# Three edits to the channel sub-layer of a decoder layer: product order in the first unit, the engine of the first partial sums, and the spacing of reloaded weights

## The chip, the cores and the metric

The kernel runs on one core of one Trainium2 chip. The metric is the device time of one execution in microseconds (us). The engines of the core are TensorE (PE, with its weight loads shown as PEld), VectorE (DVE), ScalarE (ACT), GpSimd (POOL) and SyncE (SP); each works through its own queue in order, and semaphores connect them. SP, ACT and POOL also issue DMA transfers from their queues (SPq, ACTq, POOLq). A change in time of under 0.5% (about 10.5 us here) can't be told from none.

## The reference

The kernel computes one decoder layer for a prompt of 1024 tokens and for 8 samples with one token each. A mixer sub-layer (stick-breaking attention and gated linear attention) is followed by the channel sub-layer, which the change is about:

```python
h2 = modulate(x1, sh2, sc2)
f = jnp.square(jax.nn.relu(h2 @ w_ff1)) @ w_ff2
x2 = layer_norm(ALPHA * x1 + gt2 * f, ln2_g, ln2_b)
```

The model width is 1024, `w_ff1` is 1024 x 4096 and `w_ff2` 4096 x 1024, all in float32. The 8 samples attend over a paged cache of 8192 tokens each (`cache_k`, `cache_v`, 1 MB gathers), and their layer is the same one with the same weights, so each sample passes through the mixer, then through the channel sub-layer.

## The kernel before, in words

Products. A float32 product is made as three products of a rounded high part and a low part: high by high, low by high, high by low. `three(terms)` (L485) lists them for a list of terms, one kind after the other: all high by high, then all low by high, then all high by low. `mm` (L341) records every matmul, `turn` (L367) every transpose on TensorE, and one wrapper (L212) every operation of the other engines, so that nearly all rows of the profile carry one of these three lines, and tiles tell them apart.

The prompt runs through the channel sub-layer in two halves of 512 rows: `ffn(0, ...)`, then `ffn(1, ...)` (L1578). `second_in` (L1547) makes the input of a half: eight blocks h2 of 128 x 512. For each, four transposes into `pT2`, one DVE operation that writes the modulated block, an ACT operation that writes its high part, and a POOL operation that writes its low part. The hidden width of 4096 is cut into 32 units of 128 columns. `up` (L1670) multiplies the eight blocks by a unit's weights: 24 matmuls into one PSUM tile `pmm`, then ReLU on ACT (`rl`), square on DVE, and the split into `hidh` and `hidl`. Two units make a group, and `down_tile` (L1715) multiplies a group by its rows of `w_ff2`: for each of 4 row blocks t and 2 column halves cc a sum of 6 products, in the PSUM tile `pz` (cc = 0) or `ptr` (cc = 1). `add_up` (L1735) brings each such sum into the eight running sums `f[t][cc]`: the first group's by an ACT copy, the later ones by a DVE addition. The tiles `f` come from a ring of eight buffers, so the first sums of `ffn(1)` go where the finished rows of `ffn(0)` were, once these have been stored. `finish` (L1811) normalises a row block and stores it: in `ffn(0)` by DVE and a store from ACT's queue, in `ffn(1)` by POOL (for t = 3 by DVE) and a store from SP's queue.

Weights are loaded through SP's queue into a ring of six raw buffers (`raw`, `N_RAW`), split by ACT (high) and POOL (low).

The samples. Their attention over the cache runs beside all of this as small tasks: per task a 1 MB gather of keys on POOL's queue, a multiply and a reduce on DVE (`kt`, `z`), for values eight small matmuls (`va`). When it is done, their input `h2s` is made. From then on each pair of units that `ffn(1)` loads is also used for the samples (`smp_up` L1606, `smp_sum` L1595, `smp_down` L1621): 16 matmuls with a unit pair's `w_ff1` columns (`cT` in the rows), a sum over partitions (`sel`), the squared ReLU (`hs`), and 8 matmuls into the tile `pfs`. Pairs that the prompt passed before that time are missed, and `smp_late` (L1633) loads their weights again: for each missed pair two loads `wfs` of `w_ff1`, an estimated pause, two loads `wfs2` of `w_ff2`, a pause, then the products. `smp_end` (L1760) waits until all 16 pairs are summed, then copies `pfs`, multiplies by the selector, adds the residual, normalises the 8 rows `srow` and stores `out_y_sample`.

What sets the order: the program is recorded by generators that take turns under a clock of the kernel's own (`Flow`, L45; every `yield x` stands for x us, stretched by `SCALE` = 1.2). This clock runs on estimates when the program is built, and so decides in which order each engine's instructions stand, and also how many pairs count as missed (`range(u)` in `load_up`). On the chip each queue then runs in that order.

## Time and profile before

| | |
|---|---|
| three runs | 2112.74 us median (2105.89 to 2117.82) |
| the profiled execution | 2098.6 us, span of its instructions 2096.9 us |
| TensorE busy / VectorE / GpSimd / ScalarE | 93% / 71% / 42% / 34% of the span |
| mean granted TensorE clock | 0.962 |
| chain that ended last, by engine | PE 57%, DVE 17%, DMA 13%, issue 6%, ACT 4%, POOL 2% |
| reloads `wfs` and `wfs2` | 36 loads of 512 KB (18 units, nine pairs) |

How to read it: the page is of one execution, which was 14 us faster than the median of the three others; durations and places below are of that execution. `ffn(0)` begins at about 1132 us of the span, `ffn(1)` has its first sums at about 1652 us, the last prompt product ends at about 2077 us, and the span ends at 2096.9 us. In the rows of a timeline a start and a duration are followed by engine, line, operation, output<-inputs and count, and in brackets the idle time of the engine before it and what ended it.

### The profile page before, as it was taken

To read this page: it belongs to the slowest core of one execution; us is meant where nothing else is said; L and a number is where in the kernel's file an instruction comes from. 1 tells how busy PE (TensorE), PEld (TensorE's weight loads), DVE (VectorE), ACT (ScalarE), POOL (GpSimd) and SP (SyncE) were. 2 spreads that over 40 slices of the span, in tenths; PEclk is the share of its full clock that TensorE was granted. 3 is DMA by queue.
4 is the path that set the end of the run, shared out by engine and by line. 5 is a ranking of instruction groups with operands and counts; after the bars stand their busy time and mean duration, and the time that the engine had idled before them with its cause. 6 is when DMAs were issued, how large, how long until landed. Compare 5 with 4: busy or idle time off the path is not lost.

```text
span 2096.9 us, 28831 instructions
## 1 busy us (share of the span) xinstructions
PE 1942.7 (93%) x11300; PEld 1376.2 (66%) x11300; DVE 1497.7 (71%) x1796; ACT 706.6 (34%) x1152; POOL 876.4 (42%) x597
## 2 busy tenths in 40 slices
PE   5899999999999899998998889999998999999997
PEld 2676765666656676677777656767675666677774
DVE  6568877798867588667898878887897533533357
ACT  2325444454444543222322423232222522322222
POOL 2232233334323223364466536555454644323324
PEclk9899999999999799998999999999999999999998
DMA  7785678777757558897797858787886866545554
GB/s 254 249 290 172 214 244 280 273 236 253 256 198 247 180 178 315 318 329 289 241 335 246 286 211 288 262 306 256 278 299 233 274 229 212 179 122 151 151 175 149
DMA packets 279554, 506.45 MB, mean 242 GB/s; under 512 B 16261, under 2 KB 207077, under 8 KB 243578
## 3 DMA queue, kind: packets, MB, share of 16 engines
q0 software_dynamic: 36864, 268.45, 35.2%
q1 hardware_dynamic: 215010, 207.56, 31.6%
q10 hardware_dynamic: 27544, 28.59, 3.9%
q8 instruction: 89, 1.46, 0.3%
q14 instruction: 47, 0.39, 0.1%
HBM read 473.84 MB, written 30.71 MB: 241 GB/s over the span
## 4 chain that ended last, share of the span: by engine, by line
PE 57%; DVE 17%; DMA 13%; issue 6%; ACT 4%; POOL 2%; SPq 1%; ACTq 0%; DVEq 0%; POOLq 0%
PE pmm L341 23%; PE pz L341 8%; PE ptr L341 7%; PE pbig L341 6%; PE va L341 4%; DMA vt<-in_cache_v,idx 3%; DMA wf<-in_w_ff 3%; DVE kt L212 2%; DVE z L212 2%; PE pfs L341 2%; DVE f L212 2%; DVE kp L212 2%; DVE xr L212 1%; PE paT L367 1%; PE po L341 1%
## 5 line engine op out<-in xcount | busy, mean ns | idle before, releaser
L212 DVE TENSOR_TENSOR kt<-kt,qb 128x2048 f32<-128x2048 f32 x128 | 291.4, 2278 | 26.7 <-DMA kt<-in_cache_k,idx 25.7
L212 DVE TENSOR_REDUCE z<-kt 128x32 f32<-128x2048 f32 x128 | 291.8, 2281 | 1.7
L341 PE MATMUL pmm<-h,wfh 128*128 128x512 f32 x1024 | 264.4, 404 | 3.7 <-ACT h L212 3.7
L341 PEld LDWEIGHTS pmm<-h,wfh 128*128 128x128 f32 x1024 | 190.7, 190 | 78.8 <-issue 32.4
L212 POOL DMA_INDIRECT vt<-in_cache_v,idx x128 | 133.1, 1040 | 242.7 <-PE va L341 100.9
L212 POOL TENSOR_TENSOR wfl<-wf,wfh 128x1024 fp32r<-128x1024 f32 x64 | 153.9, 2405 | 179.2 <-ACT wfh L212 91.0
L212 POOL DMA_INDIRECT kt<-in_cache_k,idx x128 | 129.8, 1014 | 217.0 <-PE va L341 72.5
L212 POOL TENSOR_TENSOR wf2l<-wf,wf2h 128x1024 fp32r<-128x1024 f32 x62 | 153.0, 2478 | 129.4 <-ACT wf2h L212 120.5
L341 PE MATMUL va<-vt,wT 128*8 128x512 f32 x1024 | 140.4, 622 | 19.0 <-DMA vt<-in_cache_v,idx 18.9
L212 ACT ACTIVATE wfh<-wf 128x1024 fp32r<-128x1024 f32 x64 | 67.7, 1057 | 236.8 <-PE pmm L341 153.9
L212 DVE TENSOR_TENSOR rl<-rl,pmm 128x512 f32<-128x512 f32 x64 | 43.7, 682 | 142.6 <-ACT rl L212 142.6
L341 PE MATMUL pmm<-hhl,wbrh 128*128 128x512 f32 x512 | 141.7, 412 | 0.6 <-DVE ke L212 0.6
L341 PE MATMUL pmm<-h,wfl 128*128 128x512 f32 x512 | 132.7, 398 | 0.0
L341 PEld LDWEIGHTS pmm<-h,wfl 128*128 128x128 f32 x512 | 96.6, 190 | 28.2 <-issue 6.8
L341 PEld LDWEIGHTS pmm<-hhl,wbrh 128*128 128x128 f32 x512 | 91.8, 191 | 34.9 <-issue 18.5
L212 DVE TENSOR_TENSOR f<-f,ptr 128x512 f32<-128x512 f32 x104 | 70.9, 682 | 49.6 <-PE ptr L341 49.5
L212 DVE TENSOR_TENSOR hidl<-rl,hidh 128x512 fp32r<-128x512 f32 x64 | 83.6, 1307 | 31.7 <-ACT hidh L212 30.2
L341 PE MATMUL pz<-wf2h,hidh 128*128 128x512 f32 x248 | 85.6, 421 | 17.8 <-ACT f L212 8.5
L212 DVE TENSOR_TENSOR_SCAN kp<-kp,zcol 128x512 f32<-128x512 f32 (+3 forms) x96 | 98.8, 1043 | 2.7 <-ACT kp L212 1.7
L212 DVE TENSOR_TENSOR f<-f,pz 128x512 f32<-128x512 f32 x104 | 70.9, 681 | 36.2 <-PE pz L341 36.0
L341 PE MATMUL ptr<-wf2h,hidh 128*128 128x512 f32 x248 | 83.8, 418 | 4.5 <-DVE f L212 3.4
L212 ACT ACTIVATE rl<-pmm 128x512 f32<-128x512 f32 x64 | 38.0, 594 | 147.5 <-PE pmm L341 143.4
(376 smaller groups left out, 3972.1 us busy)
## 6 DMA issues: line engine op xcount, KB each, us to landing
wf<-in_w_ff SPq DMA_DIRECT2D x128, 512.0 KB
ra<-in_w_ada SPq DMA_DIRECT2D x24, 1024.0 KB
wfs<-in_w_ff SPq DMA_DIRECT2D x36, 512.0 KB
wbr<-in_w_in SPq DMA_DIRECT2D x16, 512.0 KB
d_br<-brg ACTq DMA_DIRECT2D x32, 256.0 KB
g<-d_br SPq DMA_DIRECT2D x32, 256.0 KB
wo<-in_w_o SPq DMA_DIRECT2D x16, 512.0 KB
xt<-in_x_prompt SPq DMA_DIRECT2D x8, 512.0 KB
```

Source lines behind the costliest of these rows:

```text
L212: ins = f(*a, **k)
L341: ins = E.matmul(out, lhsT, rhs, start=start, stop=stop, **kw)
L367: E.transpose(out, in_, idn)
```

## The change

Three edits.

1. In `smp_late` the two pauses of 10.0 per missed pair become 6.5 (12 and 7.8 us of the kernel's own clock).
2. In `up`, unit 0 of each half lists its 24 products block by block: for each of the eight blocks high by high, low by high, high by low. The other 31 units stay as they were.
3. `add_up` takes the column half cc, and the first sums with cc = 1 are copied by DVE instead of ACT.

```diff
--- before.py
+++ after.py
@@ -1635,7 +1635,7 @@
                 rs = [raw([P, 8, P], "wfs") for y in range(2)]
                 for y in range(2):
                     Y.dma_start(rs[y], w_cols(w_ff1, P * (u + y), P))
-                yield 10.0
+                yield 6.5
                 go = []
                 flow.spawn(smp_up(rs, go))
                 rs = [raw([P, 2, 512], "wfs2") for y in range(2)]
@@ -1643,7 +1643,7 @@
                     Y.dma_start(
                         rs[y], w_ff2[P * (u + y) : P * (u + y) + P, :].rearrange("p (a b) -> p a b", a=2)
                     )
-                yield 10.0
+                yield 6.5
                 yield lambda: bool(go) and until(*rs, *go)()
                 smp_down(rs, go)
                 yield 1.0
@@ -1669,7 +1669,9 @@
 
         def up(u, wh, wl):
             p = p_mm()
-            steps = three([(h2[k], (wh[:, k, :], wl[:, k, :])) for k in range(8)])
+            terms = [(h2[k], (wh[:, k, :], wl[:, k, :])) for k in range(8)]
+
+            steps = three(terms) if u else [x for y in terms for x in three([y])]
             for x, (h, wt) in enumerate(steps):
                 mm(p, wt, h, start=x == 0, stop=x == 23)
                 if x % 6 == 5 and x < 23:
@@ -1732,9 +1734,9 @@
                 yield 1.5
 
 
-        def add_up(f, p, first):
+        def add_up(f, p, first, cc):
             if first:
-                S.activation(f, p, AF.Copy)
+                V.tensor_copy(f, p) if cc else S.activation(f, p, AF.Copy)
             else:
                 V.tensor_tensor(f, f, p, ALU.add)
 
@@ -1799,7 +1801,7 @@
                         if x > NU // 2 - 3:
                             gated(f[t][cc], gt_t[cc], p)
                         else:
-                            add_up(f[t][cc], p, x == 0)
+                            add_up(f[t][cc], p, x == 0, cc)
                         yield
             if x == NU // 2 - 3 and us is not None:
                 flow.spawn(residual())
```

Since the order of the program follows the estimated clock, more rows move than these lines say. Three places follow.

On PE, at the first unit of `ffn(0)`, before (pmm_9996 and pmm_10070 are units 0 and 1, h2_9979 is the last of the eight input blocks, pT2_9972 its transposes):

```order
L341 MATMUL pmm_10070<-h2_9915,wfh_9986 128x512
L367 MATMUL pT2_9972<-ident_133,x1_9809 128x128
L367 MATMUL pT2_9972<-ident_133,x1_9812 128x128
L367 MATMUL pT2_9972<-ident_133,x1_9815 128x128
L367 MATMUL pT2_9972<-ident_133,x1_9818 128x128
L341 MATMUL pmm_9996<-h2_9947,wfh_9782 128x512
L341 MATMUL pmm_10070<-h2_9947,wfh_9986 128x512
L341 MATMUL pmm_9996<-h2_9965,wfh_9782 128x512
L341 MATMUL pmm_10070<-h2_9965,wfh_9986 128x512
L341 MATMUL pmm_9996<-h2_9979,wfh_9782 128x512
L341 MATMUL pmm_9996<-h2_9711,wfh_9782 128x512
```

The same place after (pmm_10056 is unit 1 there):

```order
L341 MATMUL pmm_10056<-h2_9711,wfh_9986 128x512
L341 MATMUL pmm_9996<-h2_9947,wfh_9782 128x512
L341 MATMUL pmm_9996<-h2_9947,wfl_9783 128x512
L341 MATMUL pmm_9996<-h2_9965,wfh_9782 128x512 x2
L341 MATMUL pmm_9996<-h2_9965,wfl_9783 128x512
L341 MATMUL pmm_10056<-h2_9738,wfh_9986 128x512
L341 MATMUL pmm_10056<-h2_9777,wfh_9986 128x512
L341 MATMUL pmm_10056<-h2_9806,wfh_9986 128x512
L341 MATMUL pmm_10056<-h2_9915,wfh_9986 128x512
L341 MATMUL pmm_10056<-h2_9947,wfh_9986 128x512
L341 MATMUL pmm_10056<-h2_9965,wfh_9986 128x512
L341 MATMUL pmm_9996<-h2_9979,wfh_9782 128x512
```

Before, 14 products of the channel sub-layer stand ahead of the first one that reads the last block h2_9979, ten of them ahead of its transposes. After, 28 do, 11 of them ahead of the transposes, and they include low-part products (wfl) of the first unit. The next short products of the samples' attention (posT) stand behind 58 products before and 52 after.

On ACT, the first sums of `ffn(0)`, before:

```order
L212 ACTIVATE rs_10443<-mv_10441,eps_ln_148 128x1
L212 ACTIVATE f00_9950<-pz_10223 128x512
L212 ACTIVATE f01_9951<-ptr_10231 128x512
L212 ACTIVATE rs_10578<-mv_10576,eps_ln_148 128x1
L212 ACTIVATE f10_9952<-pz_10240 128x512
L212 ACTIVATE hidh_10153<-rl_10150 128x512
L212 ACTIVATE f11_9953<-ptr_10250 128x512
```

On ACT after:

```order
L212 ACTIVATE f00_9950<-pz_10234 128x512
L212 ACTIVATE wf2h_10317<-wf2_10319 128x1024
L212 ACTIVATE f10_9952<-pz_10250 128x512
L212 ACTIVATE rs_10350<-mv_10348,eps_ln_148 128x1
L212 ACTIVATE wfh_10382<-wf_10380 128x1024
L212 ACTIVATE xr_9295<-xr_9295,nm_10353,rs_10350 128x512
L212 ACTIVATE xr_9532<-xr_9532,nm_10353,rs_10350 128x512
```

On DVE after, where the other half of the first sums went:

```order
L212 BN_AGGR mv_10348<-st_10345 128x2
L212 COPY f01_9951<-ptr_10242 128x512
L212 COPY f11_9953<-ptr_10258 128x512
L212 RECIPROCAL rs_10350<-rs_10350 128x1
L212 SCALAR_TENSOR_TENSOR nm_10353<-mv_10348,rs_10350 128x1
L212 TENSOR_TENSOR xr_9295<-xr_9295,row_9283 128x512
L212 TENSOR_TENSOR xr_9295<-xr_9295,row_9287 128x512
L212 TENSOR_TENSOR kt_10074<-kt_10074,qb_8786 128x2048
L212 TENSOR_TENSOR hidl_10162<-rl_10158,hidh_10161 128x512
L212 TENSOR_REDUCE z_8785<-kt_10074 128x32
```

Four of the eight first sums (f01, f11, f21, f31) left ACT for DVE. With them the samples' work moved on DVE: between the operation that makes the last input block and the second unit's `hidl` three multiplies and four reduces of keys (kt, z) stand before, and one multiply and two reduces after; ahead of the `vz` that posT reads, one multiply, one reduce and one `hidl` fewer stand there. In `ffn(1)` the copy of f31 on DVE stands directly behind the last operation on the old tile of the same buffer, and that tile's store, on ACT's queue, lies between the two; behind the copy stand `rl` and `hidl` of the next units.

On SP, the end of the program, before (wfs are a missed pair's loads of `w_ff1`, wfs2 of `w_ff2`, srow the samples' rows):

```order
L212 DMA wfs_16653<-in_w_ff1 128x8x128
L212 DMA wfs_16654<-in_w_ff1 128x8x128
L212 DMA wfs2_16703<-in_w_ff2 128x1024
L212 DMA wfs2_16704<-in_w_ff2 128x1024
L212 DMA srow_16739<-d_x1s_130 8x1024
L212 DMA srow_16739<-d_gate1_132 8x1024
L212 DMA out_y_prompt<-f00_13231 128x512
L212 DMA out_y_prompt<-f01_13232 128x512
L212 DMA out_y_prompt<-f10_13233 128x512
L212 DMA out_y_prompt<-f11_13234 128x512
L212 DMA out_y_prompt<-f20_13235 128x512
```

After:

```order
L212 DMA wfs2_16682<-in_w_ff2 128x1024
L212 DMA srow_16755<-d_x1s_130 8x1024
L212 DMA srow_16755<-d_gate1_132 8x1024
L212 DMA out_y_prompt<-f10_13141 128x512
L212 DMA out_y_prompt<-f11_13142 128x512
L212 DMA wfs_16715<-in_w_ff1 128x8x128
L212 DMA wfs_16716<-in_w_ff1 128x8x128
L212 DMA out_y_prompt<-f20_13143 128x512
L212 DMA out_y_prompt<-f21_13144 128x512
L212 DMA wfs2_16719<-in_w_ff2 128x1024
L212 DMA wfs2_16720<-in_w_ff2 128x1024
L212 DMA out_y_prompt<-f30_13145 128x512
```

Before, the last missed pair's four loads stand ahead of all output stores. After, the last pair's first loads (wfs_16715, wfs_16716) stand behind the stores of f00 to f11, and its second loads (wfs2_16719, wfs2_16720) behind those of f20 and f21. Along PE the last product of the prompt (ptr) has one missed pair behind it before, and two after. Counted over the program, 36 such loads (nine missed pairs) become 44 (eleven), and the first missed pair stands behind 2340 of the 3072 products of the channel sub-layer before, and behind 2514 after, since the last task of the samples' attention stands 198 products later (2280 instead of 2082).

## Rows read from the trace of the kernel before

**Rows 1.** Busy time of each engine by stretch of the span: length, then PE, PEld, DVE, ACT and POOL busy (instructions), granted TensorE clock, DMA share, GB/s.

```profile
1132.00:1180.00 48.00, 39.02 (x166) 27.30 (x165) 41.30 (x43) 15.07 (x23) 28.71 (x20) 0.86 0.82 276
1180.00:1230.00 50.00, 40.74 (x165) 29.41 (x164) 41.12 (x50) 20.13 (x32) 25.50 (x13) 0.90 0.70 239
...
1900.00:2000.00 100.00, 99.39 (x680) 73.11 (x673) 40.12 (x66) 26.02 (x38) 33.45 (x14) 1.00 0.55 162
```

**Rows 2.** Timeline of PE at the start of `ffn(0)`.

```profile
1132.49 2.58 PE L341 MATMUL pmm<-h,wfh 128*128 128x512 f32 x10
1138.34 1.04 PE L367 MATMUL pT<-ident,x 128*128 128x128 f32 x4 [3.27 <-DVE h L212]
1139.03 2.06 PE L341 MATMUL pmm<-h,wfh 128*128 128x512 f32 x4
1144.83 2.50 PE L341 MATMUL pmm<-h,wfh 128*128 128x512 f32 x5 [3.74 <-ACT h L212]
1147.26 1.74 PE L341 MATMUL va<-vt,wT 128*8 128x512 f32 x8
1148.93 1.19 PE L341 MATMUL pmm<-h,wfh 128*128 128x512 f32 x4
1149.95 2.02 PE L341 MATMUL pmm<-h,wfl 128*128 128x512 f32 x8
...
1161.36 1.05 PE L341 MATMUL posT<-ones,vz 128*128 128x1 f32 x8 [1.97 <-DVE vz L212]
```

**Rows 3.** Timelines of ACT and POOL in the same stretch: the last block's high part, and the low parts of the first unit's weights and of blocks.

```profile
1144.15 0.63 ACT L212 ACTIVATE h<-h 128x512 fp32r<-128x512 f32 x1 [4.48 <-DVE h L212]
...
1121.87 2.40 POOL L212 TENSOR_TENSOR wfl<-wf,wfh 128x1024 fp32r<-128x1024 f32 x1
...
1125.39 1.29 POOL L212 TENSOR_TENSOR h<-h,h 128x512 fp32r<-128x512 f32 x1
...
1133.68 1.30 POOL L212 TENSOR_TENSOR h<-h,h 128x512 fp32r<-128x512 f32 x1
...
1144.86 1.28 POOL L212 TENSOR_TENSOR h<-h,h 128x512 fp32r<-128x512 f32 x1 [2.22 <-ACT h L212]
```

**Rows 4.** The page's groups of instructions: busy us and mean ns of one, then idle before it.

```profile
L212 DVE TENSOR_TENSOR kt<-kt,qb 128x2048 f32<-128x2048 f32 x128 | 291.4, 2278 | 26.7 <-DMA kt<-in_cache_k,idx 25.7
L212 DVE TENSOR_REDUCE z<-kt 128x32 f32<-128x2048 f32 x128 | 291.8, 2281 | 1.7
...
L212 DVE TENSOR_TENSOR f<-f,ptr 128x512 f32<-128x512 f32 x104 | 70.9, 682 | 49.6 <-PE ptr L341 49.5
```

**Rows 5.** Timelines of PE, ACT and DVE around the first sums of `ffn(0)`.

```profile
1186.39 0.80 PE L341 MATMUL pz<-wf2h,hidl 128*128 128x512 f32 x1 [2.42 <-DVE hidl L212]
...
1221.11 1.22 PE L341 MATMUL pz<-wf2h,hidh 128*128 128x512 f32 x2 [4.76 <-ACT f L212]
...
1220.45 0.60 ACT L212 ACTIVATE f<-pz 128x512 f32<-128x512 f32 x1 [1.52 <-DVE xr L212]
...
1208.89 4.19 DVE L212 TENSOR_TENSOR hidl<-rl,hidh 128x512 fp32r<-128x512 f32 x1 [1.23 <-DMA d_x<-xr]
...
1218.26 3.49 DVE L212 TENSOR_TENSOR xr<-xr,row 128x512 f32<-128x512 f32 x3 [0.88 <-ACT xr L212]
```

**Rows 6.** Timelines of PE and ACT at the first sums of `ffn(1)`.

```profile
1652.67 0.73 PE L341 MATMUL pz<-wf2h,hidh 128*128 128x512 f32 x2 [3.72 <-ACT f L212]
...
1651.63 0.34 ACTq L212 DMA_DIRECT2D out_y_prompt<-f  x1
1652.02 0.60 ACT L212 ACTIVATE f<-pz 128x512 f32<-128x512 f32 x1
```

**Rows 7.** Timelines of SP's queue and of PE in the stretch with missed pairs (wfs covers both kinds of reload, cT the products with `w_ff1`, hs those with `w_ff2`).

```profile
1951.07 1.28 SPq L212 DMA_DIRECT2D wfs<-in_w_ff  x2
...
1964.16 2.24 SPq L212 DMA_DIRECT2D wfs<-in_w_ff  x2
...
1979.01 1.01 SPq L212 DMA_DIRECT2D wfs<-in_w_ff  x2
...
1968.79 1.08 PE L341 MATMUL pfs<-wfs,cT 128*32 128x128 f32 x32
...
1980.46 1.06 PE L341 MATMUL pfs<-wfs,hs 128*32 128x512 f32 x8
```

**Rows 8.** Timelines of PE, SP's queue and POOL at the end of the span.

```profile
2076.63 0.62 PE L341 MATMUL ptr<-wwl,hidh 128*128 128x512 f32 x2
2077.18 1.08 PE L341 MATMUL pfs<-wfs,cT 128*32 128x128 f32 x32
...
2080.78 1.93 PE L341 MATMUL pfs<-wfs,hs 128*32 128x512 f32 x8 [1.17 <-DVE hs L212]
...
2068.21 17.62 SPq L212 DMA_DIRECT2D out_y_prompt<-f  x8
2092.98 1.61 SPq L212 DMA_DIRECT2D out_y_sample<-srow  x2
...
2065.19 11.75 POOL L212 TENSOR_TENSOR f<-f,row 128x512 f32<-128x512 f32 x8 [10.36 <-ACT f L212]
2077.89 6.38 POOL L212 TENSOR_TENSOR f<-f,row 128x512 f32<-128x512 f32 x4 [0.94 <-ACT f L212]
```

**Rows 9.** From the chain of waits that ended last: one weight load from its issue to the matmul that it released.

```profile
2035.68 6.53 DMA wf<-in_w_ff
```

## The prediction

> **What bounds the kernel now.** I read the busy shares first: TensorE works for 93% of the span, so a gain has to come out of places where it waits or runs slowly, or out of the stretch behind its last product for the prompt. The busy time by stretch shows where these places are [rows 1]: from 1132 to 1230 us PE works 39.02 of 48 and 40.74 of 50 us and its granted clock is 0.86 and 0.90, while from 1900 to 2000 us it works 99.39 of 100. The first stretch is the beginning of `ffn(0)`. There DVE is as busy as PE (41.30 of 48 us), so the stretch has two bounds that alternate.
>
> Next I read PE's timeline there. Before the last input block, PE does ten products, waits 3.27 us, does the block's transposes and four products, and waits 3.74 us for the block's high part [rows 2]. The second wait ends when ACT has made that part at 1144.78 (1144.15 + 0.63) [rows 3]. What PE does between and behind the waits is slow: four products take 2.06 us, the five behind the second wait 2.50, so about 0.5 us each, and by 1149.95 it is 0.25 us each (eight in 2.02) [rows 2]. Those are the two levels of its clock, 1.2 and 2.4 GHz, the lower one behind idle time.
>
> Last, the end. The last prompt product ends at 2077.25 (2076.63 + 0.62); I call this E. Behind it the last missed pair's products with `w_ff1` run at once, those with `w_ff2` start at 2080.78 [rows 8], and the span ends at 2096.9. The samples, not the prompt, end the span: from the start of the last `hs` products a chain of 16.1 us (2096.9 - 2080.78) follows that no edit touches, and it begins 3.5 us behind E.
>
> **First unit block by block.** The number of products is unchanged; only what may run before the last block arrives changes: 28 instead of 14, 11 of them ahead of the transposes. The transposes wait for DVE as before, so the 3.27 us stay. The 17 products between transposes and last block do now fill the 3.74 us wait. Their inputs are there: the first unit's low weights at 1124.27 (1121.87 + 2.40), the fourth block's low part at 1126.68, the fifth's at 1134.98 [rows 3]. Before, 14 + 5 + 4 + 8 = 31 products and one `va` group were done at 1151.97 [rows 2]. After, from 1139.03, nine products at 0.5 us (4.5, what the lower clock lasted for before it rose: four in 2.06 and five in 2.50), then eight at 0.25 (2.0), end at 1145.5, when 28 are done; the last block's low part is there at 1146.14 [rows 3], so nothing waits. Three more (0.75) and the group (1.04 at full clock, 1.74 in the row, I take 1.3) give 1147.6 for the same work. The gain is 4.4 us. Bounds: 0, if the lower clock holds on, and 7.0, both waits.
>
> What stands next is posT, which waited 1.97 us for DVE's `vz` [rows 2]. Ahead of `vz` a multiply and a reduce of keys are gone, 2.28 + 2.28 us [rows 4], and PE comes to it 4.4 us earlier with six products (1.5 us) fewer before it. That is 5.9 against 4.6 plus one `hidl`, so I count the 1.97 as gone. Bounds 0 and 1.97.
>
> **Keys later on DVE.** Up to the second unit's `hidl`, DVE has two pairs of key work less: 2 x 4.56 = 9.1 us [rows 4]. PE waited 2.42 us for that `hidl` [rows 5], and arrives 6.4 us earlier. 9.1 against 6.4 + 2.42 = 8.8: the wait goes, 2.4 us. The next wait, 4.76 us, is for ACT's copies of first sums, which stand behind a normalisation that waits for DVE (`xr`, 1.52 us) [rows 5]. The copy of `pz` stays on ACT, behind the same normalisation, and PE arrives some 8.8 us earlier, DVE 9.1 us: nearly the same wait. I take 2 us of gain, between 0 and 4.76, nearer to the side where it stays. The keys are not saved but done later. From there on the work of the samples is spread over 198 more products, some 50 us at 0.25, in which DVE has room; I count that as 0, bounded by 8 us either way, about twice the largest wait of a single place.
>
> **First sums on DVE.** A copy out of PSUM takes 0.60 us on ACT [rows 6]; on DVE the nearest row is the addition that also reads a second operand, 0.68 us [rows 4]. Eight copies of 0.6 leave ACT, eight of 0.68 join DVE, 2.7 us per half, within a group of 48 products of 12 us. PE makes a sum in 6 x 0.25 = 1.5 us, so neither engine's rate bounds it. What counts is the queue. DVE can be stretched: a `hidl`, no larger than the addition of 0.68 us [rows 4], took 4.19 us in one place [rows 5]. *The Trainium skill, "SBUF — State Buffer", section "Who interferes with whom", states that a DVE instruction with at most one SBUF input, outside the two-port modes, does not contend with GpSimd, and one with two SBUF inputs does. The `hidl` has two SBUF inputs, the copy none; by the rule the copies stay near 0.68, and by the row one of them could take 4.19. No row here shows such a copy, and the sum below takes nothing for it by either.*
>
> At the first sums of `ffn(1)` PE waits 3.72 us before, because ACT's copies stand behind the last store issue at 1651.63 [rows 6]. After, ACT's copies stand among the stores, so that wait shrinks. But f31's copy on DVE must wait until the old tile in its buffer is stored, directly behind the operation that completes it, with the next units' `rl` and `hidl` queued behind it and PE's next group behind those. I set the 3.72 saved against a wait of the same size: 0, bounds -3.7 and +4.
>
> **Missed pairs.** Closer loads would shorten the time that they need, but they start 174 products later (2514 against 2340) and there are eleven instead of nine. Before, 732 products held nine, 81 each; after, 558 hold eleven, 51 each. The four loads of a pair come every 27.9 us now (1951.07 to 1979.01) and a slot is held 17.7 and 16.3 us from issue to use [rows 7], of which a load needs 6.53 [rows 9]. I take no new wait on PE in this stretch; the bound is in the rivals.
>
> At the end, two pairs stand behind E instead of one. PE's work for one, 1.08 + 1.06 us [rows 7], moves from ahead of E to behind it: E comes 2.1 us earlier. The last pair's first loads stand behind the stores of f00 to f11. POOL ends the eight operations for these at 2076.94, E - 0.3, and the four for f20 and f21 at 2084.27, E + 7.0 [rows 8]. So the first loads leave at E and land 6.5 us later, and their products lead to `hs` in 3.6 us (2077.18 to 2080.78): E + 10.1. The second loads leave at E + 7.0 and 0.4 us later, and land at E + 13.9. The last `hs` products start there, and 16.1 us later the kernel ends: E + 30.0 instead of E + 19.65. Net 10.3 - 2.1 = +8.2 us. Bounds: +3 if POOL and the loads run faster there, since only four small products wait for the last load, and +12.
>
> **Sum.** -4.4 - 2.0 - 2.4 - 2.0 + 0 + 0 + 8.2 = -2.6 us against the profiled execution of 2098.6, so 2096.0. That execution was 14 us faster than the median of the runs, 2112.74; the same difference put there gives 2110.1. I forecast 2110.
>
> **Rivals.**
> *A, the relief carries on.* With two key pairs fewer in front, the whole 4.76 us go too, the spread of the samples' work gives its 8, and `ffn(1)`'s 3.72 are saved: -4.4 - 2.0 - 2.4 - 4.8 - 8 - 3.7 + 8.2 = -17.1, so 2096. For it: PE and DVE are almost equally busy from 1132 to 1230 [rows 1], so removing DVE work there counts. Against: the work comes back later. *The Trainium skill, "TensorEngine Tiling (Array Packing)", section "PSUM Bottleneck", advises to use both ScalarE and VectorE to empty PSUM; by it the waits of 4.76 and 3.72 us are for a drain that two engines halve, and the time would be that of A. The rows agree that PE waited for a copy on ACT, but that copy had waited for DVE or a store and itself took 0.60.*
> *B, the start gives nothing.* The clock stays low, DVE's waits move along, the 2.4 and 2.0 stay: 0 + 8.2, so 2121. For it: DVE is at 41 of 48 us [rows 1]. Against: 14 more products really are ready.
> *C, slower: the raw ring.* Missed pairs every 51 products, 51 x 0.25 + 2.1 = 15 us, or 17 with the direct pairs' work, need 4 / 17 = 0.235 slots per us, the prompt's own loads four per 96 products and its samples' work, some 28 us: 0.143. Six slots then allow a hold of 6 / 0.378 = 15.9 us, where the rows show 16.3 and 17.7; before, 6 / (4 / 27.9 + 0.143) = 21 us. From a hold above 15.9 us on, SP stops at a full ring, with the prompt's weights behind. If PE pays 1 us of the 1.8 us excess at each of eleven pairs, 11 us, and the start gives half its 10.8: -5.4 + 8.2 + 11 = +13.8, so 2127. Against: 10 us of a hold is slack between landing and use.
> *D, the end is not longer.* If the last loads are back before `hs` is ready, the pairs cost what their distance promises and the end is as before: -10.8 - 2.1, so 2100. Against: SP's order, which puts stores that wait for POOL ahead of them.
>
> **Chances.** The forecast 0.37, A 0.14, B 0.17, C 0.20, D 0.12. A difference under 0.5%, 10.5 us, can't be told from none. Faster: A's 0.14, 0.10 of D, 0.03 of the forecast, 0.27. Same: 0.31 of the forecast, 0.14 of B, 0.03 of C and 0.02 of D, 0.50. Slower: 0.17 of C, 0.03 of B and 0.03 of the forecast, 0.23. The range reaches from A, 2095, to short of C's far side, 2126. The forecast's own range is 2104 to 2118.
>
> **What would show it.** In the changed kernel's profile: PE's wait for the last block's high part gone, with the wait for the transposes still some 3 us; posT and the first `pz` without waits for DVE; a wait on DVE's f31 copy (or its absence) at the transition; two `cT` groups behind E, the last loads issued behind a store some 7 us after E, and 28 to 31 us between E and the end of the span. It is wrong if the end after E is not longer than 23 us, if PE shows waits for `wf` loads from 1900 us on, or if PE between 1230 and 1650 loses more than it gained at the start.

## The result and the profile after

| | before | after |
|---|---|---|
| median of 11 runs each, same chip | 2105.89 us (2094.11 to 2117.82) | 2133.87 us (2120.13 to 2150.17) |
| profiled execution, span | 2098.6, 2096.9 | 2133.8, 2132.0 |
| mean granted clock | 0.962 | 0.957 |

The changed kernel is slower: ratio 1.0135, 95% interval 1.0108 to 1.0163. The forecast was 2110 with a range of 2095 to 2126, and "same" as the likeliest verdict; both were missed. The medians lie 28.0 us apart, the two profiled executions 35.2, because that of the kernel before was one of its faster ones.

The page's groups answer to [rows 4]; the last one is a further one that matters below. Columns as there.

```profile
L212 DVE TENSOR_TENSOR kt<-kt,qb 128x2048 f32<-128x2048 f32 x128 | 291.3, 2278 | 33.7 <-DMA kt<-in_cache_k,idx 33.6
...
L341 PE MATMUL va<-vt,wT 128*8 128x512 f32 x1024 | 145.7, 637 | 29.5 <-DMA vt<-in_cache_v,idx 29.5
```

The key work itself costs what it did; DVE waits longer for keys (33.7 us against 26.7), and PE waits 29.5 us for values.

**The stretch in marks.** To see where the time went I cut both traces at the same points of the program. T0 is the first product of `ffn(0)`. DVE's additions `f<-f,ptr` come in 26 sets of four, 13 in each half; m1 is the end of the first set, and so on, so m14 is the first of `ffn(1)`. E is the end of the last prompt product. Lengths in us (from the timelines):

| | T0 at | T0-m1 | m1-m7 | m7-m13 | m13-m14 | m14-m17 | m17-E | E-end | T0-m14 |
|---|---|---|---|---|---|---|---|---|---|
| before | 1132.5 | 104.2 | 154.0 | 176.5 | 122.4 | 84.3 | 303.3 | 19.7 | 557.2 |
| after | 1134.0 | 93.3 | 178.8 | 174.7 | 120.8 | 80.7 | 323.1 | 26.7 | 567.5 |
| difference | +1.5 | -10.9 | +24.8 | -1.8 | -1.6 | -3.6 | +19.8 | +7.0 | +10.3 |

The start gains 10.9 us, and the next six sets lose 24.8. Of the 19.8 between m17 and E about half is work that only moved: 48 value products more stand between T0 and m14 in the kernel before (400 against 352), and 80 more stand between m17 and E in the one after (88 against 8). At 0.13 us each (1.04 for eight) that is 6 us less to do before m14, and 10 us more behind m17. So T0 to m14 is really worse by some 16 us, not 10.

The busy time of the stretch m1 to m7 in the two kernels, before first (columns as in [rows 1]):

```profile
1236.70:1390.70 154.00, 145.57 (x660) 102.92 (x659) 128.58 (x117) 39.10 (x49) 83.96 (x53) 0.99 0.78 274
```

```profile
1227.30:1406.10 178.80, 157.21 (x673) 109.81 (x672) 140.84 (x121) 40.91 (x51) 82.35 (x54) 0.92 0.68 238
```

PE, DVE and POOL do almost the same number of instructions (673 against 660 on PE). The DMA share falls, so this is not more work but more holes: 21.6 us without a matmul against 8.4. And PE's busy time grows by 11.6 us for 13 more instructions, with its granted clock down from 0.99 to 0.92; 145.57 us at a clock lower by that much would be some 157 (an estimate from these rows).

PE's waits between T0 and m14, summed by what was waited for (us in total, times, longest). Before:

```profile
PE pz L341 <- ACT f L212: 8.5, 2, 4.8
PE va L341 <- DMA vt<-in_cache_v,idx: 6.8, 4, 2.6
PE pz L341 <- DVE f L212: 5.0, 2, 4.6
...
PE posT L341 <- DVE vz L212: 2.7, 2, 2.0
PE ptr L341 <- DVE f L212: 2.4, 2, 1.3
```

After:

```profile
PE va L341 <- DMA vt<-in_cache_v,idx: 18.5, 7, 4.8
PE ptr L341 <- DVE f L212: 11.9, 10, 6.0
PE pz L341 <- DVE f L212: 10.5, 5, 4.9
PE pz L341 <- ACT f L212: 5.1, 2, 3.3
```

The waits that the edits aimed at did shrink (ACT's copies 8.5 to 5.1, `vz` off the list), but waits for gathered values and for DVE's additions grew by 27 us. Two of them show how such a wait comes about. The first, a weight load from the chain of waits in the window 1300 to 1335, and the timelines of ACT, DVE and PE behind it:

```profile
1314.75 13.01 DMA wf<-in_w_ff
```

```profile
1327.87 1.06 ACT L212 ACTIVATE wfh<-wf 128x1024 fp32r<-128x1024 f32 x1 [10.17 <-DMA wf<-in_w_ff]
1328.83 0.58 ACT L212 ACTIVATE rl<-pmm 128x512 f32<-128x512 f32 x1
```

```profile
1329.44 0.69 DVE L212 TENSOR_TENSOR rl<-rl,pmm 128x512 f32<-128x512 f32 x1 [10.57 <-ACT rl L212]
1330.05 0.68 DVE L212 TENSOR_TENSOR f<-f,pz 128x512 f32<-128x512 f32 x1
```

```profile
1330.78 1.22 PE L341 MATMUL pz<-wf2h,hidh 128*128 128x512 f32 x2 [4.90 <-DVE f L212]
```

A weight load takes 13.01 us, against 6.53 in [rows 9]. ACT waits 10.17 us for it with the split `wfh`; the ReLU `rl` stands behind that split in ACT's queue though its input was there; DVE's square waits 10.57 us for `rl`; an addition stands behind the square; PE wants the PSUM tile that this addition empties. Nothing on this path is long, and every queue merely keeps its order. POOL's timeline shows what shares the time of that load:

```profile
1314.27 0.95 POOL L212 DMA_INDIRECT kt<-in_cache_k,idx  x1
1315.53 0.94 POOL L212 DMA_INDIRECT vt<-in_cache_v,idx  x1 [0.31 <-issue]
1318.55 1.14 POOL L212 DMA_INDIRECT kt<-in_cache_k,idx  x1 [2.08 <-DVE z L212]
```

Three 1 MB gathers are issued within 4.3 us. That they stretched the load is my reading; the rows show the two side by side. The second place, timelines of DVE, POOL and PE:

```profile
1385.73 7.35 DVE L212 TENSOR_TENSOR hidl<-rl,hidh 128x512 fp32r<-128x512 f32 x1 [1.78 <-ACT hidh L212]
```

```profile
1385.46 2.43 POOL L212 TENSOR_TENSOR wf2l<-wf,wf2h 128x1024 fp32r<-128x1024 f32 x1
1387.84 2.39 POOL L212 TENSOR_TENSOR wfl<-wf,wfh 128x1024 fp32r<-128x1024 f32 x1
1390.19 2.33 POOL L212 TENSOR_TENSOR wf2l<-wf,wf2h 128x1024 fp32r<-128x1024 f32 x1
```

```profile
1395.93 1.22 PE L341 MATMUL ptr<-wf2h,hidh 128*128 128x512 f32 x2 [5.97 <-DVE f L212]
```

A `hidl` ends only when three POOL operations back to back are done, 7.35 us; PE pays 5.97.

Only one of these two places belongs to the order. e23_no_pause, a run of the next section, has the same sequence of instructions on every engine from T0 past m17 as the changed kernel, and its profiled execution shows the first path again, with nearly the same times:

```profile
1319.26 12.33 DMA wf<-in_w_ff
```

```profile
1331.69 1.06 ACT L212 ACTIVATE wfh<-wf 128x1024 fp32r<-128x1024 f32 x1 [9.91 <-DMA wf<-in_w_ff]
```

```profile
1334.61 1.22 PE L341 MATMUL pz<-wf2h,hidh 128*128 128x512 f32 x2 [4.64 <-DVE f L212]
```

The second place is not there. The same `hidl`, in DVE's timeline of that run, begins 0.7 us before the first of the three POOL operations (1387.79) and takes its usual time, and PE waits 0.07 us instead of 5.97:

```profile
1387.06 0.69 DVE L212 TENSOR_TENSOR hidl<-rl,hidh 128x512 fp32r<-128x512 f32 x1 [0.78 <-ACT hidh L212]
```

PE's waits between T0 and m14 there:

```profile
PE va L341 <- DMA vt<-in_cache_v,idx: 18.6, 8, 5.8
PE pz L341 <- DVE f L212: 11.3, 6, 4.6
PE ptr L341 <- DVE f L212: 6.2, 8, 1.8
```

So the longer waits for values and additions come back with the order, but about 6 us of the 24.8 are of one execution. So the question for the experiments: is it one edit's own work that makes these holes, or the way in which the samples' tasks now fall against the prompt's?

### The profile page after: what moved, and what is told of

It reads as the page before. It is cut to its first block, busy times and chain, and to the rows that moved or that the text cites. A ratio compares the mean times of both kernels' runs of the same rounds, so it can differ in the third digit from the quotient of the medians.

```text
span 2132.0 us, 28856 instructions
## 1 busy us (share of the span) xinstructions
PE 1956.0 (92%) x11300; PEld 1378.0 (65%) x11300; DVE 1521.7 (71%) x1804; ACT 704.6 (33%) x1146; POOL 876.3 (41%) x597
## 4 chain that ended last, share of the span: by engine, by line
PE 50%; DMA 17%; DVE 15%; issue 9%; ACT 4%; POOL 3%; SPq 0%; POOLq 0%; ACTq 0%; DVEq 0%
PE pmm L341 19%; PE pz L341 6%; PE pbig L341 6%; PE ptr L341 5%; DMA wf<-in_w_ff 5%; DMA vt<-in_cache_v,idx 4%; PE va L341 4%; DVE kt L212 2%; DVE hidl L212 2%; DVE kp L212 2%; DVE f L212 2%; PE pfs L341 2%; DMA wq<-in_w_in 1%; PE paT L367 1%; DMA ra<-in_w_ada 1%
## 5 line engine op out<-in xcount | busy, mean ns | idle before, releaser
L212 DVE TENSOR_TENSOR kt<-kt,qb 128x2048 f32<-128x2048 f32 x128 | 291.3, 2278 | 33.7 <-DMA kt<-in_cache_k,idx 33.6
L341 PEld LDWEIGHTS pmm<-h,wfh 128*128 128x128 f32 x1024 | 189.7, 190 | 74.7 <-issue 26.5
L341 PE MATMUL va<-vt,wT 128*8 128x512 f32 x1024 | 145.7, 637 | 29.5 <-DMA vt<-in_cache_v,idx 29.5
L341 PEld LDWEIGHTS pmm<-h,wfl 128*128 128x128 f32 x512 | 95.3, 189 | 32.0 <-issue 10.7
L341 PEld LDWEIGHTS pmm<-hhl,wbrh 128*128 128x128 f32 x512 | 91.8, 191 | 34.9 <-issue 18.5
L212 DVE TENSOR_TENSOR hidl<-rl,hidh 128x512 fp32r<-128x512 f32 x64 | 89.5, 1398 | 34.0 <-ACT hidh L212 25.6
L341 PE MATMUL pz<-wf2h,hidh 128*128 128x512 f32 x248 | 85.4, 423 | 15.7 <-DVE f L212 10.5
L212 ACT ACTIVATE wf2h<-wf 128x1024 fp32r<-128x1024 f32 x62 | 64.9, 1053 | 82.0 <-DMA wf<-in_w_ff 48.6
```

The lines of the kernel that those rows point to most:

```text
L212: ins = f(*a, **k)
L341: ins = E.matmul(out, lhsT, rhs, start=start, stop=stop, **kw)
```

## The experiments

All ratios are to the kernel before, run beside it on the same chip. Where lengths are given, they are of one profiled execution, cut at the marks above. Two pairs show how far executions of one order differ. Edit 1 alone leaves the order of the first 2322 products as it was: its m1-m7 is 155.1 against 154.0, its T0-m14 559.3 against 557.2. e23_no_pause has the order of the changed kernel for the first 2514 products: its m1-m7 is 170.4 against 178.8, its T0-m14 560.2 against 567.5. So a difference of less than some 8 us between two stages can be chance, and the loss of m1-m7 is 15 to 25 us.

**Each edit alone, and two without the third.**

e1_pause has only the first change below (at both places), e2_blocks only the second, e3_copies only the third, e23_no_pause the second and the third.

```diff
-yield 10.0
+yield 6.5
...
-steps = three([(h2[k], (wh[:, k, :], wl[:, k, :])) for k in range(8)])
+steps = three(terms) if u else [x for y in terms for x in three([y])]
...
-S.activation(f, p, AF.Copy)
+V.tensor_copy(f, p) if cc else S.activation(f, p, AF.Copy)
```

> Only the shorter pauses of the missed pairs. The order then holds nine missed pairs as before, starting at product 2322, and none behind the last prompt product. Theory 1 (the loss comes from the samples' attention being ordered later by edits 2 and 3 together): 6 to 12 us faster than before, near 2097, since the end after the last prompt product falls from 19.7 to some 12 to 14 us. Theory 2 (closer reloads starve the prompt's weights in the raw ring): slower than before by 8 us or more, with waits of PE for wf from 1850 us on.

> Only the first unit block by block. The samples' attention ends at product 2148 instead of 2082, missed pairs stay nine. Theory 1: within 6 us of before (a start gain of some 9 us, part of it lost again between 1230 and 1650 us). Theory 3 (the block order alone moves the keys so that DVE and the loads miss each other): slower by 15 to 25 us, with first sums of group 7 of the first half already later than before.

> Only the first sums with cc = 1 copied by DVE. The samples' attention ends at product 2064, eight missed pairs, none behind the last prompt product. Theory 1: as fast as before or up to 10 us faster. Theory 4 (copies on DVE stall its queue, at the transition to the second half above all): slower by 8 us or more, and the loss stands between the last sum of the first half and the first group of the second.

> Edits 2 and 3 without the shorter pauses. The samples' attention ends at product 2280, eleven missed pairs, as in the changed kernel, but with pauses of 10.0, so five to six pairs stand behind the last prompt product. Theory 1: as slow as the changed kernel up to the last prompt product (some 28 us late) and an end longer by two to three more pairs, so 2140 to 2165. Theory 2 (raw ring) alone: the prompt's part is as before, only the end is longer, 2115 to 2130.

| | median | ratio | T0-m1 | m1-m7 | m7-m13 | T0-m14 | E-end |
|---|---|---|---|---|---|---|---|
| e1_pause | 2110.17 | 1.004 [1.000, 1.008] | 107.0 | 155.1 | 176.2 | 559.3 | 15.2 |
| e2_blocks | 2124.14 | 1.0084 [1.0047, 1.0122] | 100.9 | 165.2 | 189.1 | 571.8 | 19.3 |
| e3_copies | 2126.17 | 1.012 [1.0065, 1.0175] | 109.6 | 151.5 | 192.1 | 581.5 | 17.7 |
| e23_no_pause | 2146.12 | 1.0236 [1.0179, 1.0292] | 94.0 | 170.4 | 175.1 | 560.2 | 48.1 |

The second edit gains 3.3 us at the start and loses 23.8 in the next twelve sets. The third loses 15.6 us between m7 and m13, in sets where it changes no instruction; another 5.4 stand in T0-m1 and 5.9 in m13-m14 (128.3 against 122.4), the two stages that hold its copies. So more than half of either loss, not all, stands where the edit's instructions aren't. Both together have the changed kernel's order up to m17, and their T0-m14 of 560.2 is of their fastest execution (2131.70 us, of six); behind E they have about five pairs of reloads, 48.1 us of end. The first edit brings that down to 26.7 in the changed kernel; alone it brings all pairs ahead of E, and E-end falls by 4.5, but m17-E grows by 7.9 (311.2 against 303.3), so it gains nothing.

Against the expectations: e1_pause didn't gain the 6 to 12 us of theory 1, and PE showed no new waits for weights (theory 2). e2_blocks came out as theory 3 had it. e3_copies lost more than theory 4's 8 us, but most of it not where that theory put it. The time of e23_no_pause lies in theory 1's range, though in its profiled execution E came only 5 us later than before, not 28.

**A shift without any edit.** If the alignment decides and not the edits' own work, then moving the samples' tasks a little must do the same to the kernel before. `K_PACE` holds the distance of the key tasks on the kernel's own clock; its fourth number is that of `ffn(0)`.

```diff
-K_PACE, K_CALM = (12.0, 11.5, 14.0, 9.0, 8.0), 3.5
+K_PACE, K_CALM = (12.0, 11.5, 14.0, 9.5, 8.0), 3.5
```

`b_` is the kernel before, `a_` the changed one; 95 stands for 9.5 and 85 for 8.5.

> The kernel before, without any of the three edits; only the pace of the samples' tasks while ffn(0) runs is 9.5 instead of 9.0 in the kernel's own clock. The order still has nine missed pairs, one behind the last prompt product, and the samples' attention ends at product 2088 (2082 before); what moves is where its tasks stand against the prompt's groups in ffn(0). Theory 5 (the kernel before has a lucky alignment in ffn(0), and edits 2 and 3 cost because they shift it, not by what they do): slower than before by 8 to 25 us, lost between the first group of ffn(0) and the first of ffn(1). Theory 6 (the DVE copies and the block order cost by themselves): within 6 us of before.

> As the run before it, with a pace of 8.5: the samples' attention ends at product 2082, nine missed pairs, one behind the last prompt product. Theory 5: slower than before by 5 to 25 us. Theory 6: within 6 us of before.

> All three edits, with the pace of 9.5 in ffn(0). The samples' attention ends at product 2142 instead of 2280, nine missed pairs instead of eleven, none behind the last prompt product. Theory 5: the end after the last prompt product falls from 26.7 to some 15 us as in the run with the pauses alone, and ffn(0) falls somewhere between the kernels before and after: 2100 to 2125. Theory 6: ffn(0) as slow as after or slower, and only the end is shorter: 2120 to 2130.

> All three edits, with the pace of 8.5: the samples' attention ends at product 2202, ten missed pairs, none behind the last prompt product. Theory 5: 2100 to 2130 with an end of some 15 us. Theory 6: 2120 to 2130.

| | median | ratio | T0-m14 | E-end |
|---|---|---|---|---|
| b_pace95 | 2137.85 | 1.017 [1.0131, 1.0208] | 592.9 | 19.3 |
| b_pace85 | 2105.23 | 0.9984 [0.9955, 1.0013] | 553.5 | 19.3 |
| a_pace95 | 2127.16 | 1.0085 [1.0055, 1.0116] | 568.6 | 15.2 |
| a_pace85 | 2125.55 | 1.0101 [1.0064, 1.0138] | 567.9 | 15.8 |

Half a microsecond of the kernel's own clock, with no work added, makes the kernel before 1.7% slower; the same step to the other side costs nothing. PE's waits from T0 to m14 in b_pace95:

```profile
PE pz L341 <- DVE f L212: 16.0, 7, 3.0
PE va L341 <- DMA vt<-in_cache_v,idx: 13.0, 6, 4.4
PE pz L341 <- ACT f L212: 11.5, 2, 6.6
PE pcol L341 <- DVE nat L212: 7.1, 2, 5.7
```

The same two kinds grow as in the changed kernel. The two versions of the changed kernel have no long end (15.2 and 15.8 us), and are still about 1% slower, so the end was not the larger part of the loss.

The theories come out mixed here. b_pace95 lost even more than theory 5's 8 to 25 us; b_pace85 lost nothing, as theory 6 had it and theory 5 had not; both versions of the changed kernel lie in theory 6's 2120 to 2130. So a shift alone can cost as much as the change did. That edits 2 and 3 cost nothing by themselves is not shown: at each of three paces the changed kernel was 0.85% to 1.35% slower than the kernel before, while the latter, moved to 8.5 and 9.5, was 0.16% faster and 1.7% slower.

**Thinner key tasks.** If the tasks' distance is the lever, wide pauses in `ffn(0)` should let the start's gain stand.

```diff
-K_PACE, K_CALM = (12.0, 11.5, 14.0, 9.0, 8.0), 3.5
+K_PACE, K_CALM = (12.0, 11.5, 14.0, 18.0, 6.0), 3.5
```

> The kernel before, with the samples' tasks paced at 18 instead of 9 while ffn(0) runs and at 6 instead of 8 in ffn(1): half as many gathers and key products beside ffn(0), the rest later. Thirteen missed pairs, nine or ten of them behind the last prompt product, so the whole is slow, some 2150 to 2200; it is the partner of the next run. All theories: from the first product of ffn(0) to its 13th group clearly shorter than the 435 us of before (104.2 + 154.0 + 176.5), near 400.

> The changed kernel with the same paces, 18 in ffn(0) and 6 in ffn(1). Thirteen missed pairs, seven or eight behind the last prompt product. Its order of the samples' tasks is nearly that of the run before it (the tasks end behind products 52, 1170, 1950, 2286, 2520 here, 58, 1162, 1938, 2274, 2520 there). Theory 5 (only the alignment costs): with half the samples' work beside ffn(0) the edits cost nothing there, and from the first product of ffn(0) to its 13th group it is 3 to 12 us shorter than its partner. Theory 6 (the DVE copies and block order cost by themselves): as long as its partner's or up to 15 us longer, and the difference stands at the first groups.

Measured: 2170.63, 1.0323 [1.0281, 1.0365], and 2176.24, 1.036 [1.032, 1.0399]. Both pay for the work that is then left for later (E-end 74.7 and 62.8). T0-m13 is 392.8 and 397.2. The changed kernel leads by 2 to 8 us up to the tenth set, loses that in the next two and ends T0-m13 4.4 us behind, where theory 5 had it 3 to 12 us ahead. This is in theory 6's range, though not at the first groups, where that theory put it, and it is less than two executions of one order can differ. With thinner keys T0-m1 is 94.7 in the kernel before and 92.8 in the changed one, 1.9 us apart instead of 10.9. The first unit is done 4 us earlier there too (16.1 us behind T0 against 20.1), but half of that is lost again by m1. That fits a gain at the start that is in good part key work put off; it is a reading.

**Positions near those of before.** With edits 1 and 2, two distances give an order whose tasks stand close to those of before. As a measure of that I counted how many of the 3072 prompt products of the sub-layer stand ahead of each `posT` step, of which five fall among them:

```
before        58   744  1331  1758  2082
changed       52   840  1590  1956  2280
e12_pace94    52   722  1318  1770  2094
e12_pace87    52   816  1352  1758  2082
```

```diff
-K_PACE, K_CALM = (12.0, 11.5, 14.0, 9.0, 8.0), 3.5
+K_PACE, K_CALM = (12.0, 11.5, 14.0, 9.4, 8.0), 3.5
...
-K_PACE, K_CALM = (12.0, 11.5, 14.0, 9.0, 8.0), 3.5
+K_PACE, K_CALM = (12.0, 11.5, 14.0, 8.7, 8.0), 3.5
```

> First unit block by block and the shorter pauses, first sums all on ACT as before, and the pace of 9.4 in ffn(0), chosen because the samples' tasks then end behind products 52, 722, 1318, 1770, 2094, close to the 58, 744, 1331, 1758, 2082 of the kernel before; nine missed pairs, none behind the last prompt product. Theory 5: with the alignment restored the start gain of 3 to 10 us shows, 2092 to 2106. Theory 7 (the block order costs by itself, through the low parts that it needs early): 2115 to 2130.

> As the run before it with a pace of 8.7: tasks end behind products 52, 816, 1352, 1758, 2082, nine missed pairs, none behind the last prompt product. Theory 5: the first task ends 72 products later than before, so some of the gain is lost in ffn(0): 2095 to 2120. Theory 7: 2115 to 2130.

Measured: 2137.21, 1.0173 [1.014, 1.0206], T0-m14 582.1; and 2114.54, 1.0054 [1.0027, 1.0081], T0-m14 559.9. The first is as bad as the worst shift, far above both theories' ranges, though its positions are near those of before, so the idea that these positions tell the time fell. What counts is finer than they can show. The second lies in theory 5's range, and just below theory 7's.

**Which resource gives no slack.** Two relief runs, each for both kernels. Light keys: from `ffn(0)` on the multiply and the reduce of keys work on a quarter of each tile. Half gathers: from there on each gather moves 0.5 MB, other rows, and the amount of DVE and PE work is kept, but each multiply and each reduce of keys is cut into two pieces, of 1.21 us instead of 2.28.

```diff
-dot = V.tensor_tensor(k3, k3, qb[:, None, :].to_broadcast([P, 4, 512]), ALU.mult)
+dot = V.tensor_tensor(k3[:, 0:R], k3[:, 0:R], qb[:, None, :].to_broadcast([P, R, 512]), ALU.mult)
...
-G.indirect_dma_start(t, None, src, off)
+nc.gpsimd.indirect_dma_start(t[:, 0:1024], None, short[name], off)
```

> The kernel before; from ffn(0) on the multiply and reduce of keys work on a quarter of each gathered tile (the samples' attention is not computed fully), so each takes some 0.7 us instead of 2.28; gathers, products and the order stay (tasks end behind products 38, 744, 1326, 1758, 2082). Partner of the next run. If DVE's key work carries the waits (theory 8): from the first product of ffn(0) to the first group of ffn(1) 520 to 540 us instead of 557, 2075 to 2090 in all. If the gathers' traffic does (theory 9): 550 to 560 us, 2095 to 2110.

> The changed kernel with the same quarter of the key work on DVE (the samples' attention is not computed fully); tasks end behind 52, 840, 1590, 1956, 2280 as in the changed kernel. Theory 8: the stretch from the first product of ffn(0) to the first group of ffn(1) is as short as its partner's or up to 10 us shorter, where it is 10 us longer with full key work (567.5 to 557.1). Theory 9: still some 10 us longer than its partner.

> The kernel before; from ffn(0) on each gather fetches half a tile (0.5 instead of 1 MB; the samples' attention reads other rows and uses the half twice, so it isn't the reference's), DVE and PE do as much as before, the multiply and the reduce in two pieces each; the order stays (38, 744, 1326, 1758, 2082). Theory 8: 550 to 565 us from the first product of ffn(0) to the first group of ffn(1). Theory 9: 530 to 545 us, PE's waits for gathers and the ACT waits for weights mostly gone.

> The changed kernel with half gathers in the same way (samples' attention from other rows), order of the changed kernel (52, 840, 1590, 1956, 2280). Theory 8: still some 10 us longer than its partner in that stretch. Theory 9: as short as its partner's or up to 10 us shorter.

| | median | ratio | T0-m14 | after minus before there |
|---|---|---|---|---|
| full work | 2105.89, 2133.87 | 1.0135 [1.0108, 1.0163] | 557.2, 567.5 | +10.3 |
| b_light_keys | 2085.95 | 0.9951 [0.9923, 0.9978] | 538.6 | |
| a_light_keys | 2107.88 | 1.0029 [0.9994, 1.0064] | 532.4 | -6.2 |
| b_half_gathers | 2096.91 | 1.0009 [0.9983, 1.0036] | 550.3 | |
| a_half_gathers | 2104.82 | 1.0007 [0.9978, 1.0035] | 539.5 | -10.8 |

With either one relieved, the changed kernel is the shorter one from T0 to m14, and with the gathers halved no difference can be told in the whole: 1.0007 against 1.0009. The 48 value products that the changed kernel has fewer there (6 us) must be set against these lengths too, which leaves 0 and -5. In m1-m7, where the loss stood, the changed kernel is 6.2 us longer with light keys (162.2 against 156.0) and 2.5 with half gathers (154.3 against 151.9), where it was 24.8. For the kernel before, halving the gathered bytes moves the time by nothing that can be measured and T0-m14 by 6.9 us; for the changed one T0-m14 falls by 28.0. The busy time and PE's waits from T0 to m14 in a_half_gathers (whose wrappers stand two or one lines lower):

```profile
1145.60:1685.10 539.50, 500.13 (x2231) 354.78 (x2229) 473.30 (x548) 163.94 (x217) 295.87 (x176) 0.97 0.56 179
```

```profile
PE va L343 <- DMA vt<-in_cache_v,idx: 7.1, 3, 2.8
PE pz L343 <- POOL wf2l L213: 5.5, 3, 3.0
PE pz L343 <- DVE f L213: 5.3, 4, 2.3
```

The waits for values (18.5) and for additions (`pz` 10.5) are back near what the kernel before has. DVE is no less busy here than in the changed kernel with full gathers (473.30 us, against 463.38), so the amount of DVE's work alone was not the bound. Of the theories neither holds by itself: theory 8 had the light keys right in both kernels and b_half_gathers, theory 9 a_half_gathers.

Two things besides the bytes changed in the half gathers, and keep them from showing that it was the traffic. In DVE's queue other operations now stand between the two pieces of 46 of 80 key operations from T0 to m14 (44 in a_half_gathers), so an addition has less to wait for there. And the order is not that of the partner: the first posT of the kernel before moved from behind 58 products to behind 38, in both relief runs, and of POOL's 182 instructions between T0 and m14 at most 153 are in the sequence of before in b_half_gathers, where b_pace95, the shift alone, keeps 149. With light keys the changed kernel stays about 1% behind its partner in the time (2107.88 against 2085.95): its end is 26.9 us long, and the moved value products come behind m14, as above.

**The other two bad orders with half gathers.** If the same cause stands behind the shift and behind edit 3, they must be relieved too.

b_pace95_half and e3_half are b_pace95 and e3_copies, each with the half gathers above added:

```diff
-G.indirect_dma_start(t, None, src, off)
+nc.gpsimd.indirect_dma_start(t[:, 0:1024], None, short[name], off)
```

> The kernel before with the pace of 9.5 in ffn(0) (1.7% slower than before with full gathers, 592.9 us between the first product of ffn(0) and the first group of ffn(1)) and half gathers from ffn(0) on (0.5 instead of 1 MB, other rows for the samples). Theory 9 (a shifted order costs because gathers and weights, with DVE, leave no slack): the stretch is 540 to 560 us and the whole 2092 to 2108. Otherwise 575 us or more and 2115 or more.

> Only the first sums with cc = 1 copied by DVE, with half gathers from ffn(0) on (other rows for the samples). With full gathers the stretch was 581.5 us and the whole 1.2% slower than before. Theory 9: 540 to 560 us, whole 2090 to 2105. If the copies cost by themselves (theory 6): 565 us or more, whole 2110 or more.

| | ratio, full gathers | ratio, half | T0-m14, full | half |
|---|---|---|---|---|
| b_pace95 | 1.017 [1.0131, 1.0208] | 1.0033 [1.0, 1.0065] | 592.9 | 563.7 |
| e3_copies | 1.012 [1.0065, 1.0175] | 1.0034 [1.0002, 1.0066] | 581.5 | 559.2 |

Most of either loss goes, 29 and 22 us, but T0-m14 stays 13 and 9 us above b_half_gathers' 550.3. In b_pace95_half one wait for DVE's `nat` of 7.7 us is left, in e3_half one of 7.5 us for `tmpf`; what remains was not settled. Against the expectations, b_pace95_half lies just above theory 9's ranges (563.7 and 2110.53), and e3_half has theory 9's stretch but a time (2110.78) at the edge of theory 6's. Still, four orders that lie from 0 to 1.7% above the kernel before with full gathers lie within 0.3% of each other with half of them, which is unlikely to come of new orders alone. Whether the fewer bytes or the finer pieces on DVE did it was not tried apart.

## Why the prediction was wrong

*The last block's wait.* Right. PE's timeline of the changed kernel at the start answers to [rows 2]:

```profile
1139.88 0.91 PE L367 MATMUL pT<-ident,x 128*128 128x128 f32 x4 [3.04 <-DVE h L212]
...
1146.37 0.96 PE L341 MATMUL pmm<-h,wfh 128*128 128x512 f32 x3 [0.30 <-ACT h L212]
1147.73 0.50 PE L341 MATMUL pmm<-h,wfh 128*128 128x512 f32 x1 [0.41 <-POOL h L212]
...
1148.40 1.04 PE L341 MATMUL va<-vt,wT 128*8 128x512 f32 x8
...
1156.00 1.05 PE L341 MATMUL posT<-ones,vz 128*128 128x1 f32 x8
...
1178.31 1.87 PE L341 MATMUL va<-vt,wT 128*8 128x512 f32 x2 [4.44 <-DMA vt<-in_cache_v,idx]
```

The transposes still wait 3 us, and the 3.74 us became 0.30 and 0.41. By the end of that `va` group, 15.4 us behind T0, 33 products and the group are done, where 31 and a group took 19.5 [rows 2]: with 0.5 us for the two more products a gain of 4.6, forecast 4.4. posT doesn't wait and starts 22.0 us behind T0 instead of 28.9, but that was luck: the prediction's own figures (PE 5.9 us earlier at a wait of 1.97, DVE earlier by 4.6 and a `hidl` of 0.68) leave a wait of 2.6 us. In the traces `vz` is ready 6.9 us earlier, since that `hidl` had taken 2.03 us, and PE comes 5.0 earlier. Rival B fell.

*The `hidl` and first sums of `ffn(0)`.* The wait for the `hidl` is gone, and the first sums wait 3.28 us for ACT at 1209.08 instead of 4.76 [rows 5]; in between stands a wait for values that the sum had not (4.44, above). The start's total, -10.9 to m1 where the terms made -10.8, is right in part by luck. The busy time from T0 to m1, before first (columns as in [rows 1]):

```profile
1132.49:1236.70 104.21, 85.97 (x357) 60.73 (x356) 87.92 (x100) 38.12 (x56) 54.64 (x34) 0.89 0.71 241
```

```profile
1134.00:1227.30 93.30, 81.28 (x331) 57.82 (x330) 76.67 (x96) 34.03 (x51) 52.33 (x31) 0.91 0.68 231
```

PE's time without a matmul falls by 6.2 us (18.2 to 12.0). The other 4.7 are busy time: 26 matmuls, 16 of them value products, now stand behind m1.

*Keys later on DVE, "I count that as 0, bounded by 8 us either way".* This step failed. It asked whether DVE has room in the mean over the stretch. It has, but that isn't the question: the samples' gathers, key work and value products stand among the prompt's weight loads, splits and additions in fixed queues, and each task that falls at a new place can hold up a load or an addition. The loss was 24.8 us from m1 to m7 (16.4 in e23_no_pause, the same order), and some 16 from T0 to m14 with the start's gain taken off and the moved work put back (9 in e23_no_pause). It is the prediction's own last sign of being wrong: PE lost more between 1230 and 1650 than it had gained at the start. What the runs show in its place: a shift of the tasks without any edit cost 1.7%; more than half of what edits 2 and 3 lost alone lies in sets that they don't touch; and with lighter key work or half gathers the loss from m1 to m7 fell to 6.2 and 2.5 us. Together this makes the changed alignment the likely cause. It is not shown that no part is the edits' own work, as no version of the changed kernel came as low as the kernel before with full gathers and keys; nor which resource it is, as the half gathers changed the order and DVE's pieces too. The path by a late weight load, ACT's split, `rl` and an addition is seen in two executions of the order; it was not tried by itself. Rival A, which counted on 8 us of gain from the same spread, had the sign wrong.

*First sums on DVE.* The copies went as priced: the one at the transition took 0.69 us. So did its wait for the store, in DVE's and PE's timelines:

```profile
1683.86 0.69 DVE L212 COPY f<-ptr 128x512 f32<-128x512 f32 x1 [4.57 <-DMA out_y_prompt<-f]
```

```profile
1668.19 0.73 PE L341 MATMUL pz<-wf2h,hidh 128*128 128x512 f32 x2 [1.84 <-ACT f L212]
```

3.72 us [rows 6] became 1.84, against 4.57 on DVE, where another copy waited 3.47 for its store; m13-m14 is 1.6 shorter. Setting them off against each other was right there. As an edit alone it still costs 1.2%, more than half of it away from the copies. *The Trainium skill, "SBUF — State Buffer", section "Who interferes with whom", has a DVE instruction with at most one SBUF input stay clear of GpSimd outside the two-port modes, and one with two contend with a GpSimd instruction that reads SBUF. The trace agrees in both: the eight copies took 0.68 or 0.69 us though POOL operations overlapped five of them, and a `hidl` took 7.35 beside three POOL operations. In the Trainium skill, "TensorEngine Tiling (Array Packing)", section "PSUM Bottleneck", the advice is to empty PSUM with two engines; in e3_copies that gave no gain: PE's waits for ACT's copies were 7.4 us from T0 to m14, against 8.5 before.*

*Missed pairs.* Right that PE wouldn't wait for them, so rival C fell: PE's waits from 1900 us to E are these. The 2.7 us for weight loads were 1.2 in the kernel before.

```profile
PE pfs L341 <- DMA wf<-in_w_ff: 2.7, 6, 0.7
PE pz L341 <- DVE hidl L212: 1.9, 1, 1.9
```

*The end.* Right in mechanism, a little too large. SP's and PE's timelines answer to [rows 8], with E at 2105.3 (2104.64 + 0.63):

```profile
2103.93 1.14 SPq L212 DMA_DIRECT2D wfs<-in_w_ff  x2
2107.31 3.79 SPq L212 DMA_DIRECT2D out_y_prompt<-f  x2
2111.19 0.88 SPq L212 DMA_DIRECT2D wfs<-in_w_ff  x2
```

```profile
2104.64 0.63 PE L341 MATMUL ptr<-wwl,hidh 128*128 128x512 f32 x2
...
2116.01 3.11 PE L341 MATMUL pfs<-wfs,hs 128*32 128x512 f32 x8 [1.89 <-DMA wfs<-in_w_ff]
```

The last loads leave 5.9 us behind E, not 7.4, behind two stores as foreseen; their products start at E + 10.7 instead of E + 13.9, with 16.0 us behind them (16.1 foreseen). E to the end is 26.7, forecast 30.0 and at least 28, so 7.0 instead of 10.3 more. Rival D fell.

So of the difference of 35.2 us between the two profiled executions, 10.9 less at the start and 7.0 more at the end were foreseen. The rest was not: 24.8 from m1 to m7, some 10 of value products that moved behind m17, and 1.5 ahead of T0, where nothing was changed; m7 to m17 came out 7.0 shorter, about as much as the work that moved out of it. Since one pair fewer stands ahead of E, about 2 us, some 11 of the 19.8 from m17 to E are left without a cause. No version tried that does the whole work is faster than the kernel before by more than can be measured; the best is b_pace85 at 0.9984.

## What to carry to other kernels

In a stretch where several in-order queues are 70 to 95% busy, a wait that is removed locally says little about the time: whatever the edit shifts behind it meets other things, and room in the mean doesn't price that. Before such an edit is credited or blamed, shift the same tasks a little without it; if that alone moves the time by as much, the edit was not measured. Compare stages from a mark inside the program, with the work that moved across the marks counted, since executions of one kernel start the same stage up to 20 us apart. And profile the same order twice before a single hole is explained: here a hole of 6 us was gone the second time. A relief run is no cleaner than an edit if it moves the order too.
